# A hybrid attention and delta-rule layer on one core: early embedding and x loads, per-tile normalisation, scan scaling on ACT, and another slab order

## The chip, the core and the metric

The kernel runs on one core of a Trainium2 chip. A core has five engines, each with an in-order instruction queue of its own: TensorE (PE) multiplies matrices, VectorE (DVE), ScalarE (ACT) and GpSimd (POOL) work element by element, and SyncE (SP) issues transfers. They wait for each other through semaphores. The metric is the device time of one execution in microseconds (us); the kernel before takes 786.01 us (median of three runs, 785.57 to 786.49). Everything is in fp32.

## The reference

One layer, sequence 512 and width 1024, batch 1. What is computed, cut to its lines:

```python
h = rms_norm(x, norm_pre)
aq, ak, av, az, dq, dk, dv, db, da, dz, gA, gB = split(h @ w_in)
q = rope(rms_norm(aq, q_norm)); k = rope(rms_norm(ak, k_norm))   # 8 query, 2 key heads of 128
y_att = (softmax(q k^T / sqrt(128)) av * silu(az)) @ w_br_att
cq, ck, cv = silu(short_conv([dq, dk, dv], conv_w))               # 8 heads of 128
g = -exp(a_log) * softplus(da + dt_bias); beta = sigmoid(db)      # forward and backward
o_dn = delta_rule(l2(cq)/sqrt(128), l2(ck), cv, g, beta)          # chunks of 64, both directions summed
y_dn = (rms_norm(o_dn, dn_norm) * silu(dz)) @ w_br_dn             # norm per head
mix = (sigmoid(gA) * y_att + sigmoid(gB) * y_dn) @ w_out
x = x + rms_norm(mix, norm_post)
e = p @ w_ple_proj                                                # the embedding: p is 512 x 256
x = x + rms_norm(sigmoid(x @ w_ple_gate) * e, ple_norm)
```

## The kernel before

**Precision and slabs.** Each fp32 operand is split into a high part, rounded by a cast, and the rest. A product is three matmuls: high by low, low by high, high by high. The combined projection is cut into *slabs* of 128 output columns (dq0 to dq7, dk, dv, dz, az, gA, gB, and later ydn and yatt) and into *blocks* of 512 columns (kv, q0, q1, out0, out1, pg0, pg1). A slab is 8 k-tiles of 3 matmuls over 512 tokens, 24 matmuls (`gemm_t`, L475 to L477). A block's weights come in four pieces, of 24 matmuls each (`gemm_k`, L513 to L515). For each slab and piece `fetch` issues one 512 KB transfer into `wraw`, then ACT casts it into `whi` (1024 columns), and POOL, or DVE, subtracts to get `wlo`. There are two buffers of each of the three. PE's first matmul of a slab reads `wlo` and so waits for all three steps.

**The planner.** The program is written by a planner that runs in Python (class `Flow`, L36 to L130). Every part of the layer is a generator that asks for buffers, events or times; the planner keeps a clock and one list of planned occupied stretches for each engine, always continues the ready part with the smallest priority number (table `PR`), and issues instructions in the planned order, all through L101. Helpers give each instruction its planned duration: `A` for ACT, `V` for DVE, `G` for POOL, `W` for DVE with POOL kept free, `Q` for a transfer. `stream`, the last in priority, works through the slabs in the order of the table `ORDER` and fills whatever PE time the other parts leave. `split` decides by two constants (`COOL`, `HOT`) whether DVE or POOL does a subtraction. What the planner decides is only the order in each queue; on the chip every instruction runs when its semaphores allow.

**The start.** `first_loads` issues the transfers on SP: the norm row, half of p, half of w_ple_proj (`wpp`), the other halves, then the four tiles x0 to x3. `warm_up` (L1708) runs transposes of the identity on PE to fill the time. `h_part` broadcasts the norm row by four matmuls (L347), then squares each x tile on ACT with its sum, takes the inverse root on POOL (`st`), scales with two DVE instructions per tile, and only after all four tiles does it go on to transpose (L374). `ple_part` transposes p (L1171), casts, and runs the product with wpp as eight groups of six matmuls (L1186 to L1188), whose results go to DRAM until the end of the layer.

**The decay and its exponentials.** `decay` (L603 to L676) projects db and da, sums the log decays over a chunk with transposes (L662) and writes the sums to DRAM (`CI`). `prep(g, d)`, for head group g and direction d, reads CI back broadcast over the partitions, masks it on POOL, and takes exponentials on ACT: eight 128x64 activations for each of four chunks (L840), 128 in all. Later it scales them (L860). `make_tables` builds the rope tables on POOL and DVE as soon as the decay is done.

**The scan.** Two groups of four heads run one after the other: `phase_a` (kk and qk products, L884 and L889, and the forward substitution), `phase_b` (the steps in both directions, L1041 to L1093) and `phase_y`. `phase_y(g)` takes the scan output `o` (4 tiles of 128x512, in units `u`), squares it on ACT, sums per head on DVE into `so`, takes the inverse root on POOL (a power with 16 columns, L264, tile `kinv`), scales `o` by it with four 128x512 DVE instructions, and then transposes each head on PE (L1151) and multiplies by the norm weight and the SiLU gate. While it does so, `stream` feeds PE: in group 1 with block q0.

Of the kernel before, what the change touches and what calls it, by code (L numbers as in the profile page):

```python
# [16 lines left out]
NT = 4  # L17
D = 1024
# [120 lines left out]
gB5 dq1 dq2 dk1 dk2 dk6 dq0 dk0 dk3 dq3 dk5 dk7 gB1 dq5 dv0 az4  # L139
dv3 dz2 gB6 gB4 gA1 gB3 dz3 dq4 dv1 dv2 az0 dq7 dz4 dz1 dk4 dq6  # L140
az3 dz7 dz0 dv4 az7 dv5 gA6 gA4 dz6 az6 gB0 kv gB7 dv7 gA7 dv6
gA5 dz5 az2 az5 gA2 q0 gA0 ydn1 q1 gA3 az1 gB2 free_h ydn0 ydn2 ydn6
ydn7 ydn4 ydn5 ydn3 yatt6 yatt4 yatt3 yatt1 vec yatt7 yatt0 yatt5 yatt2 out0 out1 pg0
# [12 lines left out]
def layer(ctx, tc, x, p, wt, wba, wn, wpp, npre, rows, qkn, hd16, npost, pnorm, dnorm, cs, out):  # L156
# [20 lines left out]
    def Q(kb, dep, o, i):  # L177

        t = op("DGE", 0.46, dep, sync.dma_start, o, i)
        return op("DMA", kb * 0.364, t + 0.5, None) + 1.0  # L180
# [111 lines left out]
    def first_loads():  # L292
        yield "get", "u15"
        ple["p"] = unit(15, [128, 4, 256])
        ple["tp"] = []

        def p_half(i):
            ple["tp"].append(Q(2, 0.0, ple["p"][:, 2 * i:2 * i + 2], p[256 * i:256 * i + 256].rearrange("(t p) n -> p t n", p=128)))

        xu = []  # L300

        def ple_weights(half):
            raw = tile("wraw", [128, 2, 512])
            load["ple", half] = raw, Q(4, 0.0, raw, wpp.rearrange("(j p) n -> p j n", p=128)[:, :, half * 512:half * 512 + 512])
            fetched["ple", half].set(F.now)
# [11 lines left out]
        p_half(0)  # L317
        ple_weights(0)
        p_half(1)
# [16 lines left out]
    def h_part():  # L336
# [15 lines left out]
        yield "get", "blk"  # L352
        junk = tile("blk", [128, D])
        for t in range(NT):
            xt, tx = load["x", t]
            ts = A(1.05, tx, act.activation, junk, xt, AF.Square, accum_out=st[:, t:t + 1])
            tj = ts
            ts = rsqrt(1, ts, st[:, t:t + 1], 1.0 / D, EPS)
            for half in range(2):
                xh = xt[:, half * 512:half * 512 + 512]  # L360
                sc[t, half] = ts = V(0.68, max(ts, tn), dve.scalar_tensor_tensor, out=xh, in0=xh, scalar=st[:, t:t + 1],
                                     in1=nb[half], op0=ALU.mult, op1=ALU.mult)
        free("blk", tj)
        free("mm", ts)
        free("mm", ts)
        for t in range(NT):
            xt = load["x", t][0]
            for half in range(2):
                yield "at", sc[t, half] + 0.3
                yield "get", "aux"  # L370
                pt = bank("aux", [128, 4, 128])
                for j in range(4):
                    k = half * 4 + j
                    pe.transpose(pt[:, j, :], xt[:, k * 128:(k + 1) * 128], ident)  # L374
                yield "pe", 0.45
                cc = slice(t * 128, (t + 1) * 128)
                _, te = split(pt, hTh[half][:, :, cc], hTl[half][:, :, cc], F.now, 512)
# [17 lines left out]
        return t  # L395

# [419 lines left out]
    def prep(g, d):  # L816
# [12 lines left out]
        for c in range(NT):  # L829
# [12 lines left out]
            t = A(1.6, t, exps)  # L842
# [284 lines left out]
    def phase_y(g, be):  # L1127
# [9 lines left out]
        for c in range(NT):  # L1137
            t = W(0.62, t, dve.tensor_mul, o[:, c], o[:, c], bc(f[:, c]))
# [22 lines left out]
    def ple_part():  # L1161
# [4 lines left out]
        for t_ in range(NT):  # L1166
            yield "at", ple["tp"][t_ // 2] + 0.2
# [38 lines left out]
    def make_tables():  # L1206

        yield "ev", dec_ev
# [576 lines left out]
def _layout(inputs):  # L1785
# [28 lines left out]
    return {"x": f["x"][0], "p": f["p"][0, 0], "wt": wt, "wba": wba, "wn": wn, "wpp": f["w_ple_proj"][0],  # L1814
# [20 lines left out]
```

## Time and profile before

| what | value |
|---|---|
| median of three runs | 786.01 us (785.57 to 786.49) |
| the profiled execution | 786.52 us |
| its span, first to last instruction | 784.8 us |
| mean granted clock of PE | 0.988 |
| busy: PE / DVE / ACT / POOL | 97% / 60% / 45% / 39% |
| weight casts on ACT | 84, 1050 ns each |
| weight subtractions on POOL | 70, 2401 ns each |
| exponentials on ACT (L840) | 128, 31.7 us in all |

A row of the timeline gives start, duration, engine, line, operation, output and input tiles, shape and count; in brackets the idle time before it and what ended that. A row of the waits gives the waiting instruction, what it waited for, then the sum in us, the number of waits and the longest. A row of windows gives the stretch, its length, the busy time of PE, its weight loads, DVE, ACT and POOL (with instructions), the granted clock as a share of the full one, the DMA share and GB/s. A tile's row gives the shortest, median and longest duration in ns, and the first and last start. Durations of PE's matmuls overlap: what counts there is the step from start to start.

### The profile page before, as it was taken

To read this page: it belongs to the slowest core of one execution; us is meant where nothing else is said; L and a number is where in the kernel's file an instruction comes from. 1 tells how busy PE (TensorE), PEld (TensorE's weight loads), DVE (VectorE), ACT (ScalarE), POOL (GpSimd) and SP (SyncE) were. 2 spreads that over 40 slices of the span, in tenths; PEclk is the share of its full clock that TensorE was granted. 3 is DMA by queue.
4 is the path that set the end of the run, shared out by engine and by line. 5 is a ranking of instruction groups with operands and counts; after the bars stand their busy time and mean duration, and the time that the engine had idled before them with its cause. 6 is when DMAs were issued, how large, how long until landed. Compare 5 with 4: busy or idle time off the path is not lost.

```text
span 784.8 us, 11964 instructions
## 1 busy us (share of the span) xinstructions
PE 760.5 (97%) x4542; PEld 634.1 (81%) x4542; DVE 469.3 (60%) x906; ACT 353.1 (45%) x693; POOL 306.6 (39%) x275
## 2 busy tenths in 40 slices
PE   9999999999999999999999998999999999999995
PEld 6777788788788888888788876787888888888885
DVE  5426868797854769895944554617666744313434
ACT  6568567734441463325432232324557633342422
POOL 4245566303212463203521242656437444562411
PEclk9998999999999999999999998999999999999998
DMA  8362345646202133755231233324233345643313
GB/s 290 123 197 81 134 135 153 196 161 161 95 28 81 54 135 114 208 152 131 98 106 41 81 97 106 121 80 148 81 122 130 116 152 221 228 142 153 94 42 133
DMA packets 54555, 100.51 MB, mean 128 GB/s; under 512 B 21025, under 2 KB 22497, under 8 KB 54498
## 3 DMA queue, kind: packets, MB, share of 16 engines
q1 hardware_dynamic: 54498, 99.75, 39.5%
q8 instruction: 36, 0.59, 0.3%
q14 instruction: 21, 0.17, 0.1%
HBM read 80.83 MB, written 18.91 MB: 127 GB/s over the span
## 4 chain that ended last, share of the span: by engine, by line
PE 70%; DVE 4%; ACT 3%; POOL 2%; issue 2%; DMA 1%; POOLq 0%; DVEq 0%; ACTq 0%; SPq 0%
PE mm L475 12%; PE mm L477 12%; PE mm L476 12%; PE mm L497 4%; PE mm L495 4%; PE mm L496 4%; PE aux L1061 2%; PE mm L1409 2%; PE mm L513 2%; PE mm L514 2%; PE mm L515 2%; PE aux L1093 2%; PE aux L1079 1%; PE aux L1041 1%; PE aux L1052 1%
## 5 line engine op out<-in xcount | busy, mean ns | idle before, releaser
L101 POOL TENSOR_TENSOR wlo<-wraw,whi 128x1024 fp32r<-128x1024 f32 x70 | 168.1, 2401 | 328.4 <-ACT whi L101 317.1
L475 PE MATMUL mm<-u,wlo 128*128 128x512 f32 x576 | 234.0, 406 | 7.5 <-POOL wlo L101 4.4
L477 PE MATMUL mm<-u,whi 128*128 128x512 f32 x576 | 226.2, 393 | 0.0
L476 PE MATMUL mm<-u,whi 128*128 128x512 f32 x576 | 225.6, 392 | 0.0
L101 ACT CAST whi<-wraw 128x1024 fp32r<-128x1024 f32 x84 | 88.2, 1050 | 139.9 <-PE mm L477 70.9
L475 PEld LDWEIGHTS mm<-u,wlo 128*128 128x128 f32 x576 | 109.1, 189 | 28.9 <-POOL wlo L101 6.1
L477 PEld LDWEIGHTS mm<-u,whi 128*128 128x128 f32 x576 | 108.7, 189 | 23.5
L476 PEld LDWEIGHTS mm<-u,whi 128*128 128x128 f32 x576 | 109.1, 189 | 19.9
L101 DVE SCALAR_TENSOR_TENSOR f<-mm,cw,f 128x510 f32<-128x510 f32 (+1 forms) x96 | 71.9, 749 | 34.7 <-ACT f L101 32.1
L495 PE MATMUL mm<-u,u 128*128 128x512 f32 (+1 forms) x136 | 52.0, 383 | 0.0
L497 PE MATMUL mm<-u,u 128*128 128x512 f32 (+1 forms) x136 | 51.4, 378 | 0.0
L496 PE MATMUL mm<-u,u 128*128 128x512 f32 (+1 forms) x136 | 51.2, 377 | 0.0
L101 DVE TENSOR_TENSOR u<-aux,u 128x512 f32<-128x512 f32 (+1 forms) x56 | 37.5, 688 | 20.4 <-ACT u L101 16.8
L101 POOL TENSOR_TENSOR u<-wraw,u 128x1024 fp32r<-128x1024 f32 x16 | 38.3, 2402 | 14.5 <-ACT u L101 14.3
L513 PE MATMUL mm<-whi,u 128*128 128x512 f32 x96 | 38.9, 405 | 0.0
L514 PE MATMUL mm<-wlo,u 128*128 128x512 f32 x96 | 38.3, 398 | 0.0
L515 PE MATMUL mm<-whi,u 128*128 128x512 f32 x96 | 38.2, 397 | 0.0
L101 ACT COPY c<-aux 128x512 f32<-128x512 f32 x18 | 10.6, 590 | 54.6 <-DVE f L101 30.9
L840 ACT ACTIVATE u<-u,cj 128x64 f32<-128x64 f32 x128 | 31.7, 334 | 6.5 <-POOL u L101 6.5
L101 ACT ACTIVATE f<-mm 128x512 f32<-128x512 f32 (+1 forms) x36 | 20.1, 571 | 21.4 <-PE mm L497 8.4
L497 PEld LDWEIGHTS mm<-u,u 128*128 128x128 f32 x136 | 25.6, 188 | 4.8
L496 PEld LDWEIGHTS mm<-u,u 128*128 128x128 f32 x136 | 25.6, 188 | 4.6
(245 smaller groups left out, 1260.9 us busy)
## 6 DMA issues: line engine op xcount, KB each, us to landing
wraw<-in_wt_dram SPq DMA_DIRECT2D x72, 512.0 KB, 3.4
wraw<-in_wn_dram SPq DMA_DIRECT2D x28, 512.0 KB, 4.0
u<-CI SPq DMA_DIRECT2D x16, 256.0 KB, 4.8
u<-in_x_dram SPq DMA_DIRECT2D x4, 512.0 KB, 7.6
eD<-c SPq DMA_DIRECT2D x8, 256.0 KB, 2.6
gate_gB<-go SPq DMA_DIRECT2D x8, 256.0 KB, 2.1
gate_az<-go SPq DMA_DIRECT2D x8, 256.0 KB, 2.0
gate_dz<-go SPq DMA_DIRECT2D x8, 256.0 KB, 2.3
```

The source lines that it names most:

```text
L101: fn(*a, **k)
L475: pe.matmul(o, lo[:, k, :], mh(k), start=(k == 0), stop=False)
L476: pe.matmul(o, hi[:, k, :], ml(k), start=False, stop=False)
L477: pe.matmul(o, hi[:, k, :], mh(k), start=False, stop=(k == 7))
L495: pe.matmul(o, b, hi, start=(i == 0), stop=False)
L496: pe.matmul(o, a, lo, start=False, stop=False)
L497: pe.matmul(o, a, hi, start=False, stop=(i == 7))
L513: pe.matmul(o[t], b, hi, start=(k == 0), stop=False)
L514: pe.matmul(o[t], a, lo, start=False, stop=False)
L515: pe.matmul(o[t], a, hi, start=False, stop=(k == 7))
L840: act.activation(e, e, AF.Exp, bias=cj[:, d, c, 4 * g + h, i:i + 1])
L1061: pe.matmul(pw[:, h, :], Vm[g][d][:, 4 * c + h, :], r[:, h, :], start=True, stop=True)
```

## The change

- **First loads.** p is stored so that each partition's row is one run of 4 KB and comes in one transfer; each half of wpp is stored as contiguous 4 KB rows too. SP issues: norm row, p, both halves of wpp, x0 to x3. A planned transfer now costs 0.3 us per KB of a row and 1.3 behind it, before 0.364 and 1.0.
- **x_norm.** The normalisation is a part of its own. It sets an event for each x tile, and `h_part` transposes a tile as soon as that tile is scaled.
- **phase_y.** The scaling of `o` is sixteen 128x128 activations on ACT with a scale per partition (L1141), where it was four 128x512 multiplications on DVE. The planner gives four of them 1.15 us, and eight exponentials 1.64 for 1.6.
- **Tables.** `make_tables` waits for both directions of group 0's exponentials to be scaled and no longer for the decay alone.
- **Constants.** New `ORDER`, `OUT0`, `PR`; `WARM` 8.4 for 9; `COOL` 1.5 for 2.5. The matmuls are the same in number and shape; there are 21 warm-up transposes and not 20.

```diff
 ORDER = """
-gB5 dq1 dq2 dk1 dk2 dk6 dq0 dk0 dk3 dq3 dk5 dk7 gB1 dq5 dv0 az4
+dq0 dq3 gB0 dq1 dk1 dq2 dk0 dk2 dk3 dv2 dz4 dk4 dk7 dz3 dv3 dv0
...
-PR = dict(dec=5, dm1=2, y=2, conv=1, gate=3, kv=9, q=8, head=8, ple=2, prep=9, tab=11)
+PR = dict(dec=7, dm1=11, y=4, conv=6, gate=0, kv=9, q=6, head=0, ple=11, prep=4, tab=7)
...
-WARM = 9
+WARM = 8.4
-COOL, HOT = 2.5, -3
+COOL, HOT = 1.5, -3
...
-        return op("DMA", kb * 0.364, t + 0.5, None) + 1.0
+        return op("DMA", kb * 0.3, t + 0.5, None) + 1.3
...
-            load["ple", half] = raw, Q(4, 0.0, raw, wpp.rearrange("(j p) n -> p j n", p=128)[:, :, half * 512:half * 512 + 512])
+            load["ple", half] = raw, Q(4, 0.0, raw, wpp[half])
...
-        p_half(0)
+        ple["tp"] = Q(4, 0.0, ple["p"], p)
         ple_weights(0)
-        p_half(1)
...
+        spawn(x_norm(sc, sc_ev, nb, tn), 0)
         for t in range(NT):
             xt = load["x", t][0]
+            yield "ev", sc_ev[t]
...
+    def x_norm(sc, sc_ev, nb, tn):
+        yield "get", "blk"
+        junk = tile("blk", [128, D])
+        for t in range(NT):
+            xt, tx = load["x", t]
+            yield "at", tx - 0.4
+            ts = A(1.05, tx, act.activation, junk, xt, AF.Square, accum_out=st[:, t:t + 1])
+            tj = ts
+            ts = rsqrt(1, ts, st[:, t:t + 1], 1.0 / D, EPS)
+            for half in range(2):
+                xh = xt[:, half * 512:half * 512 + 512]
+                sc[t, half] = ts = V(0.68, max(ts, tn), dve.scalar_tensor_tensor, out=xh, in0=xh, scalar=st[:, t:t + 1],
+                                     in1=nb[half], op0=ALU.mult, op1=ALU.mult)
+            sc_ev[t].set(F.now)
...
         for c in range(NT):
-            t = W(0.62, t, dve.tensor_mul, o[:, c], o[:, c], bc(f[:, c]))
+            def scaled(c=c):
+                for h in range(4):
+                    act.activation(o[:, c, h], o[:, c, h], AF.Copy, scale=f[:, c, h:h + 1])
+
+            t = A(1.15, t, scaled)
...
-        yield "ev", dec_ev
+        yield "ev", E_ev[0, 0]
+        yield "ev", E_ev[0, 1]
         yield "get", "f2"
...
-    return {"x": f["x"][0], "p": f["p"][0, 0], "wt": wt, "wba": wba, "wn": wn, "wpp": f["w_ple_proj"][0],
+    return {"x": f["x"][0], "p": f["p"][0, 0].reshape(4, 128, 256).transpose(1, 0, 2), "wt": wt, "wba": wba, "wn": wn, "wpp": f["w_ple_proj"][0].reshape(2, 128, 2, 512).transpose(2, 1, 0, 3),
```

How the queues stand at the places where the orders differ most. A row is a line of the kernel, the operation, output and input tiles and the shape; `x8` is eight alike. First ACT, at the first exponentials of group 0. In before, `whi_521` is the high part of slab dk1, `whi_570` that of dk2 and `whi_648` that of dk6:

```order
L101 CAST whi_521<-wraw_412 128x1024
L101 ACTIVATE f_78_523<-mm_459,cw 128x512
L101 ACTIVATE mm_459<-f_78_523 128x512
L840 ACTIVATE u_73_499<-u_73_499,cj 128x64 x8
L840 ACTIVATE u_74_500<-u_74_500,cj 128x64 x8
L840 ACTIVATE u_73_499<-u_73_499,cj 128x64 x8
L101 CAST whi_570<-wraw_495 128x1024
L101 ACTIVATE f_83_572<-mm_524,cw 128x512
L840 ACTIVATE u_74_500<-u_74_500,cj 128x64 x8
L101 ACTIVATE f_88_615<-mm_610 128x512
L101 CAST whi_648<-wraw_553 128x1024
```

In the changed kernel `whi_550` is the high part of dk1 and the cast behind the last row below is that of dq2 (`go_552` is a gate's activation):

```order
L841 ACTIVATE u_66_468<-u_66_468,cj 128x64 x8
L841 ACTIVATE u_67_469<-u_67_469,cj 128x64 x8
L101 CAST whi_550<-wraw_464 128x1024
L101 ACTIVATE go_552<-mm_496 128x512
L841 ACTIVATE u_66_468<-u_66_468,cj 128x64 x8
L841 ACTIVATE u_67_469<-u_67_469,cj 128x64 x8
L101 ACTIVATE f_81_593<-mm_588 128x512
L841 ACTIVATE u_66_468<-u_66_468,cj 128x64 x8
L841 ACTIVATE u_67_469<-u_67_469,cj 128x64 x8
L841 ACTIVATE u_66_468<-u_66_468,cj 128x64 x8
```

In before the 24 exponentials stand ahead of dk2's cast; now 16 stand ahead of dk1's and 40 more ahead of dq2's, and slabs dq0, dq3, gB0 and dq1 come before them. Next ACT at phase_y(1), before (`f_604` to `f_607` are the squares; `whi_4493` and `whi_4525` are pieces 3 and 4 of q0, `u_608_4445` takes the transposed heads):

```order
L101 ACTIVATE f_604_4441<-u_518_3954 128x512
L101 ACTIVATE f_605_4442<-u_518_3954 128x512
L101 ACTIVATE f_606_4443<-u_518_3954 128x512
L101 ACTIVATE f_607_4444<-u_518_3954 128x512
L101 CAST whi_4493<-wraw_4383 128x1024
L101 CAST whi_4525<-wraw_4459 128x1024
L101 CAST u_608_4445<-mm_4531 128x512
```

and now (`whi_4501` and `whi_4538` are pieces 3 and 4 of q0):

```order
L101 ACTIVATE f_604_4446<-u_524_4018 128x512
L101 ACTIVATE f_605_4447<-u_524_4018 128x512
L101 ACTIVATE f_606_4448<-u_524_4018 128x512
L101 ACTIVATE f_607_4449<-u_524_4018 128x512
L101 CAST whi_4501<-wraw_4405 128x1024
L1141 ACTIVATE u_524_4018<-u_524_4018,kinv 128x128 x16
L101 CAST whi_4538<-wraw_4485 128x1024
```

The sixteen activations stand between the casts of pieces 3 and 4. Last PE, at the first transpose of phase_y(1), before:

```order
L513 MATMUL mm_4453<-whi_4424,u_11_127 128x512
L514 MATMUL mm_4453<-wlo_4425,u_9_125 128x512
L515 MATMUL mm_4453<-whi_4424,u_9_125 128x512
L1151 MATMUL mm_4531<-ident,u_518_3954 128x128 x4
L513 MATMUL mm_4450<-whi_4493,u_12_128 128x512
L514 MATMUL mm_4450<-wlo_4494,u_10_126 128x512
```

and now:

```order
L514 MATMUL mm_4458<-whi_4501,u_12_128 128x512
L515 MATMUL mm_4458<-wlo_4502,u_10_126 128x512
L516 MATMUL mm_4458<-whi_4501,u_10_126 128x512
L1156 MATMUL mm_4580<-ident,u_524_4018 128x128 x4
L514 MATMUL mm_4455<-whi_4538,u_12_128 128x512
L515 MATMUL mm_4455<-wlo_4539,u_10_126 128x512
```

Before, the first transpose stood behind pieces 1 and 2 of q0 (48 matmuls behind the last scan step); now it stands behind piece 3 (72 of q0 and 6 of slab gB3).

More of the change, by code (lines that the diff above doesn't have):

```diff
@@ L138 @@
 ORDER = """
-gB5 dq1 dq2 dk1 dk2 dk6 dq0 dk0 dk3 dq3 dk5 dk7 gB1 dq5 dv0 az4
[L140 to L143, printed above, removed]
-pg1
-"""
-OUT0 = 'ydn5 ydn3 yatt6 yatt4'
-PR = dict(dec=5, dm1=2, y=2, conv=1, gate=3, kv=9, q=8, head=8, ple=2, prep=9, tab=11)
+dq0 dq3 gB0 dq1 dk1 dq2 dk0 dk2 dk3 dv2 dz4 dk4 dk7 dz3 dv3 dv0
+gA5 dz7 dk6 gA3 gB4 az6 dz2 az5 gA2 dv1 dq5 dq4 gA1 dk5 dq6 dq7
+dz0 az2 gA7 dz1 az0 dv7 gB1 dv4 vec az1 az3 dz5 gA0 kv dv5 gB7
+dv6 gA4 gB5 az4 gB6 gB3 q0 dz6 gA6 q1 az7 gB2 free_h ydn6 ydn4 ydn7
+ydn0 ydn2 ydn5 ydn3 ydn1 yatt0 yatt3 yatt4 yatt1 yatt2 yatt7 yatt6 yatt5 out0 out1 pg0
+pg1
+"""
+OUT0 = 'ydn7 ydn3 ydn3 yatt3'
+PR = dict(dec=7, dm1=11, y=4, conv=6, gate=0, kv=9, q=6, head=0, ple=11, prep=4, tab=7)
 GAP = 0.0
 X_DVE = ()
-WARM = 9
+WARM = 8.4
 W1 = 0
-COOL, HOT = 2.5, -3
+COOL, HOT = 1.5, -3
 @with_exitstack
@@ L294, in first_loads @@
         ple["p"] = unit(15, [128, 4, 256])
-        ple["tp"] = []
-        def p_half(i):
-            ple["tp"].append(Q(2, 0.0, ple["p"][:, 2 * i:2 * i + 2], p[256 * i:256 * i + 256].rearrange("(t p) n -> p t n", p=128)))
         xu = []
@@ L351, in h_part @@
         sc = {}
[L352 to L365, printed above, removed]
+        sc_ev = [Event() for _ in range(NT)]
+        spawn(x_norm(sc, sc_ev, nb, tn), 0)
         for t in range(NT):
             xt = load["x", t][0]
+            yield "ev", sc_ev[t]
             for half in range(2):
@@ L395, in h_part @@
         return t
+    def x_norm(sc, sc_ev, nb, tn):
[12 more added lines that the diff above has]
+            sc_ev[t].set(F.now)
+        free("blk", tj)
+        free("mm", ts)
+        free("mm", ts)
     slab, blocks, fetched = {}, {}, {}
@@ L840, in exps @@
                         act.activation(e, e, AF.Exp, bias=cj[:, d, c, 4 * g + h, i:i + 1])
-            t = A(1.6, t, exps)
+            t = A(1.64, t, exps)
             if away:
@@ L1166, in ple_part @@
         for t_ in range(NT):
-            yield "at", ple["tp"][t_ // 2] + 0.2
+            yield "at", ple["tp"] + 0.2
             yield "get", "mm"
```

## The prediction

> **What bounds the kernel now.** The page comes first, for which engine is full; then the waits of TensorE (PE), for where it is not; then windows and the timeline around the two largest waits, for who is late there. On the page:
>
> ```profile
> span 784.8 us, 11964 instructions
> PE 760.5 (97%) x4542; PEld 634.1 (81%) x4542; DVE 469.3 (60%) x906; ACT 353.1 (45%) x693; POOL 306.6 (39%) x275
> PEclk9998999999999999999999998999999999999998
> ```
>
> PE is busy for 97% of the span; no other engine reaches two thirds. The change leaves the matmuls alone but for one warm-up transpose more, so it can only add or take away time in which PE stands still, and time in which its clock is low: the PEclk row has three eights (the 4th, the 25th and the last slice). PE's waits, largest first:
>
> ```profile
> PE mm L475 <- POOL wlo L101: 4.4, 2, 3.7
> PE mm L1151 <- DVE u L101: 3.7, 3, 2.4
> PE mm L475 <- POOL saq L272: 1.9, 2, 1.2
> PE aux L972 <- issue: 1.1, 2, 0.6
> ```
>
> The two top waits are the two places where the clock falls:
>
> ```profile
> 40.00:60.00 20.00, 16.97 (x86) 13.96 (x85) 5.08 (x8) 12.65 (x44) 9.22 (x9) 0.98 0.69 193
> 60.00:80.00 20.00, 19.29 (x80) 15.71 (x81) 12.94 (x19) 16.53 (x49) 10.50 (x9) 0.85 0.27 83
> 460.00:480.00 20.00, 16.14 (x61) 12.41 (x60) 11.02 (x12) 4.88 (x7) 9.46 (x8) 0.83 0.47 152
> 59.31:66.14 6.83, 5.43 (x13) 4.26 (x14) 3.75 (x6) 6.83 (x25) 4.89 (x4) 0.50 0.33 92
> 472.32:479.15 6.83, 5.33 (x13) 4.08 (x14) 3.37 (x4) 0.58 (x1) 0.77 (x1) 0.50 0.38 122
> ```
>
> The column behind the five busy times is the granted clock, as a mean. The last two rows frame the fall: half speed for 6.83 us, of which PE had work for 5.4, so 2.7 us lost each time, beside the wait itself. **Place one**, ACT and then POOL:
>
> ```profile
> 41.94 0.27 PE L662 MATMUL aux<-ident,f 128*64 128x128 f32 x1
> 51.39 5.83 ACT L840 ACTIVATE u<-u,cj 128x64 f32<-128x64 f32 x24
> 57.13 1.03 ACT L101 CAST whi<-wraw 128x1024 fp32r<-128x1024 f32 x1
> 58.31 2.35 POOL L101 TENSOR_TENSOR wlo<-wraw,whi 128x1024 fp32r<-128x1024 f32 x1 [1.02 <-ACT whi L101]
> 60.71 0.79 PE L475 MATMUL mm<-u,wlo 128*128 128x512 f32 x1 [3.74 <-POOL wlo L101]
> ```
>
> The first row is the transpose of the summed decays, from which the exponentials' inputs go through DRAM and back. The exponentials stand in ACT's in-order queue ahead of the cast of slab dk2's weights; cast and subtraction follow, and PE has waited 3.74 us. **Place two**, the per-head norm of the second scan (phase_y(1)):
>
> ```profile
> 457.25 1.16 PE L1093 MATMUL aux<-c,u 128*128 128x128 f32 x8
> 460.33 2.20 ACT L101 ACTIVATE f<-u 128x512 f32<-128x512 f32 x4 [1.48 <-DVE u L1102]
> 464.20 2.90 POOL L264 TENSOR_TENSOR kinv<-kinv,pw 128x16 f32<-128x16 f32 x1
> 467.36 2.38 POOL L101 TENSOR_TENSOR wlo<-wraw,whi 128x1024 fp32r<-128x1024 f32 x1
> 467.43 6.81 DVE L101 TENSOR_TENSOR u<-u,kinv 128x512 f32<-128x512 f32 x4 [3.97 <-POOL kinv L101]
> 470.53 2.56 POOL L101 TENSOR_TENSOR wlo<-wraw,whi 128x1024 fp32r<-128x1024 f32 x1 [0.79 <-ACT whi L101]
> 463.73 0.39 PE L513 MATMUL mm<-whi,u 128*128 128x512 f32 x1
> 468.94 0.39 PE L515 MATMUL mm<-whi,u 128*128 128x512 f32 x1
> 470.44 0.30 PE L1151 MATMUL mm<-ident,u 128*128 128x128 f32 x1 [1.11 <-DVE u L101]
> 470.95 0.33 PE L1151 MATMUL mm<-ident,u 128*128 128x128 f32 x1 [0.21 <-DVE u L101]
> 473.69 1.08 PE L1151 MATMUL mm<-ident,u 128*128 128x128 f32 x2 [2.42 <-DVE u L101]
> ```
>
> From the last scan step (457.25) on: squares, sums, a power on POOL, then four scalings on DVE in 6.81 us, of which the transposes wait for the first three; PE's cover, 48 matmuls of q0, ends before them. From 463.73 to 468.94 are 23 steps: 0.2265 us for each 128x512 matmul, 5.4 for a slab of 24.
>
> **The change, part by part.**
>
> *phase_y's scale from DVE to ACT.* Four DVE instructions go for sixteen 128x128 activations. What they cost is shown by the tile's summary (min/median/max in ns) and by sixteen activations of the same shape:
>
> ```profile
> L101 DVE TENSOR_TENSOR u<-u,kinv x8: 677/688/2878, 294.2 to 473.6; 128x512 f32<-128x512 f32 x8
> 272.11 4.77 ACT L860 ACTIVATE u<-u,Nj 128x128 f32<-128x128 f32 x16
> ```
>
> So ACT takes 4.8 us where DVE took 6.81, and would take 4 x 0.688 = 2.75 if nothing ran beside it; two of its four stretched while POOL's wlo (467.36 and 470.53) ran. [...] I take the 6.81, for POOL subtracts beside it in the new order too: the chain is 2.0 us shorter.
>
> What hides it matters more. In the new order PE has 6 matmuls of gB3 and 72 of q0 behind the last scan step before the first transpose, 78 x 0.2265 = 17.7 us against 48 x 0.2265 = 10.9; the scan step itself is 1.0 more (457.25 to 469.17, the end of the 48, less 10.9). The chain from that step on, by the rows above: 10.2 us until kinv is there (467.43 less 457.25), as before; then 4.8 of ACT: 15.0. PE comes to the transposes at 18.7: no wait, 3.7 us of slack. Also ACT's cast of q0's block 4 stands behind the sixteen: cast to 16.1, subtraction 2.4, 18.5, while PE wants it behind the first transposes, at about 19.1; block 3 is cast ahead of them and comes in time by some half a microsecond. So the 1.11+0.21+2.42 and the 0.4 of the slower steps between go, and with them the 2.7 of low clock: **-7.1 us** (bounds: 0, if the chain is 7 us later than I count, and -7.1).
>
> phase_y(0): ACT has 4 squares, 12 decay activations (12/16 x 4.77 = 3.6) and the sixteen ahead of az0's cast. From the last scan step: kinv at 10.2 and sixteen to 15.0, a cast and a subtraction (1.05 + 2.4), 18.5, or 20.5 if the twelve hold the sixteen up by 2 us. PE has 51 large matmuls until then (11.6 us) and 8.4 of small ones, 20.0. So 0 to 1.5 with the slack of a gate's activation: taken **+0.5**.
>
> *New slab order at place one.* All 64 exponentials of group 0 still run in this stretch. In ACT's new queue the cast for dk1 stands behind 16 of them, the one for dq2 behind 16+24 = 40. At 5.83/24 = 0.243 us each, from the transpose at L662 (L663 after): first exponential +9.45 (51.39 less 41.94, as before), 16 exps 3.9, cast and tanh 1.5, 16 exps 3.9, a square 0.5, 24 exps 5.8, cast 1.05, subtraction with a mask step ahead of it 2.7: +28.7. PE has until then the rest of dq3, gB0, dq1, dk1 (2.0 + 3 x 5.4 = 18.3), 18 matmuls of the embedding (4.1) and some 2.5 of small ones and transposes: +25. It waits **3.6 us** at dq2, as it waits 3.74 at dk2 now; dk1 itself comes within 0.5 of its turn. The exchange is nearly even, clock included.
>
> *p, w_ple_proj and x at the start.* These are the rows:
>
> ```profile
> 2.88 3.78 PE L347 MATMUL mm<-blk,ones 1*128 1x512 f32 x4
> 10.97 1.06 ACT L101 ACTIVATE blk<-u 128x1024 f32<-128x1024 f32 x1
> 11.70 0.47 PE L1186 MATMUL mm<-u,u 128*128 128x512 f32 x1
> 13.97 5.35 DVE L101 SCALAR_TENSOR_TENSOR u<-u,st,mm 128x512 f32<-128x512 f32 x8
> 26.80 0.42 PE L604 MATMUL mm<-u,f 128*64 128x512 f32 x1 [0.22 <-ACT u L101]
> u<-in_x_dram SPq DMA_DIRECT2D x4, 512.0 KB, 7.6
> ```
>
> One issue fewer and longer rows bring x0 down some 1.6 us sooner, by my count of the issues. But the first square (10.97) does not wait for x0: ahead of it in ACT's queue stand the casts of p's transposes, and those wait for PE, which has 8 warm-ups (6 before) and the 3.78 us of the norm row's broadcast first. The square stays near 10.9. Thereafter the per-tile events let x0 be transposed while x3 is still to be squared, so the decay starts near 24.8 and not at 26.80: -2.0. But five of eight embedding groups are done by then; the other 18 matmuls (4.1 us) come later, and PE's idle stretches between the transposes (2.3 us) are inside the 24.8. Together **+2.1**; less 0.4 us of small stalls (0.22 in the decay row, the rest beside it) that the new fill covers: **+1.7**. Bounds: -2 (x's lead is used after all, since rows show x landing late, 7.6 us from issue) and +3.
>
> *Tables later.* make_tables leaves POOL and DVE when the group-0 exponentials need them, and comes with dz3 to dv0. In before one short wait for a subtraction remains beside the 3.7 (4.4-3.7 = 0.7, at dv3); in the new place the weights of dv3 and dv0 come 1.5 and 0.6 us ahead of PE: **-0.6** (bounds -0.7 and +1.5).
>
> *The rest of the order.* Slabs of the same size in other places: the casts and subtractions behind them are as many per slab in the scan, the attention and the output as before, so waits such as the 1.9 behind saq and the 1.1 of issue are kept at their price: **0** (bounds -2 and +2).
>
> **Sum**: -7.1 + 0.5 - 0.1 (3.6 for 3.74) + 1.7 - 0.6 = -5.6. The profiled execution ran 786.52 us (span 784.8 and 1.7 around it), the median of the runs shown is 786.01. I take the median: 786.0 - 5.5 = **780.5 us**.
>
> On the clock, since it decides 2.7 us at dq2: both long waits of before halved it, and the fall at 59.31 came 2.4 us after the wait began (60.71 less 3.74 is 56.97). [...]
>
> **The rivals.**
>
> *A: the wait at dq2 is shorter, or leaves the clock at full speed.* For it: the exponentials begin when their inputs come back from DRAM, and the head is 2 us ahead. Against: 40 of them stand before one cast. 780.5 - 2.7 = 777.8. Chance 0.2.
>
> *B: x's early landing is used.* If ACT gets to x0 at its landing, the head gains 2 instead of losing 1.7: 780.5 - 3.7 = 776.8. Against: the queue above. 0.15.
>
> *C: ACT becomes the gate (slower).* Place: the casts behind activations on ACT. If ACT's sixteen end 4.2 us later than I count at phase_y(1), block 4 of q0 uses up its 0.6 of slack, PE waits 3.6 and halves its clock again: 7.1 gained there is 6.3 given back; with az0's wait at 1.5 (1.0 above my 0.5) and 3 at the head (1.3 above): 780.5 + 6.3 + 1.0 + 1.3 = 789.1. [...] For it: a cast behind 4.8 us of activations, with 0.6 us of slack. Against: the wait must grow by a row that I have not seen. 0.18.
>
> *D: the change does not do what it says at phase_y(1).* If POOL's subtractions ahead of the power, or a cast ahead of the squares, make that chain 6 us longer, the 3.7 us of slack are gone, PE waits 2.3 and the clock falls: 780.5 + 2.3 + 2.7 = 785.5. Against: in the new queues nothing of that size stands there. 0.09.
>
> **How the numbers follow.** My forecast, within 2 us of 780.5, has 0.38. A measurement of this kernel can tell 0.2% (1.6 us) from no change. Faster: forecast, A and B, 0.38 + 0.2 + 0.15 = 0.73, less 0.01 for ends near the bound: 0.72. Same: D and that end, 0.10. Slower: C, 0.18. The range takes in B with its bound (776.8 less 2.3) and D and half of C: 774.5 to 788.
>
> **What would show it.** In the profile after: no PE wait for the transposes of phase_y(1), and full clock in the slice around 470; a wait of 3 to 4 us on wlo near 65 us with the clock low behind it; the decay's first matmul near 24.8; the first square near 10.9. Wrong would be: a long wait at q0's block 4 or az0, a first square at x0's landing (near 8.5), or a new stall of several us where I have put 0, in the scan or the attention.

## The result, and the profile after

The changed kernel takes 777.45 us (median of four runs, 777.38 to 778.91), the kernel before beside it 785.79: ratio 0.9897, 95% interval 0.988 to 0.9914, so 8.3 us less. Forecast were 5.5 us less and 780.5 (774.5 to 788.0). The profiled executions have spans of 775.7 and 784.8 us, 9.1 us apart; the profiled execution of before took 786.5 us, at the upper end of its runs, so that terms read from the two profiles add to 9.1 and not to 8.3.

The page of the changed kernel:

```profile
span 775.7 us, 11989 instructions
PE 756.2 (97%) x4543; PEld 631.2 (81%) x4543; DVE 462.5 (60%) x902; ACT 360.0 (46%) x719; POOL 302.3 (39%) x274
PEclk9999999999999999999999999999999999999998
```

The eights of the 4th and the 25th slice are gone from the clock row. PE's waits and the same windows as before:

```profile
PE mm L476 <- POOL wlo L101: 3.0, 1, 3.0
PE mm L476 <- POOL saq L272: 2.4, 2, 1.2
...
PE mm L1156 <- DVE u L101: 0.5, 1, 0.5
```

```profile
40.00:60.00 20.00, 20.00 (x95) 16.49 (x95) 6.96 (x11) 16.39 (x53) 9.65 (x10) 1.00 0.68 208
60.00:80.00 20.00, 17.03 (x72) 13.60 (x71) 11.88 (x17) 13.50 (x36) 7.13 (x3) 0.91 0.29 96
460.00:480.00 20.00, 20.00 (x93) 16.38 (x92) 3.16 (x5) 10.41 (x23) 10.95 (x8) 1.00 0.41 132
```

From 460 to 480 us PE is now busy without a gap at full clock (16.14 us at 0.83 before). One long wait is left, between 60 and 80. Here it is, on ACT, POOL and PE:

```profile
57.59 5.84 ACT L841 ACTIVATE u<-u,cj 128x64 f32<-128x64 f32 x24
63.33 1.04 ACT L101 CAST whi<-wraw 128x1024 fp32r<-128x1024 f32 x1
64.51 2.35 POOL L101 TENSOR_TENSOR wlo<-wraw,whi 128x1024 fp32r<-128x1024 f32 x1 [6.74 <-ACT whi L101]
66.91 0.50 PE L476 MATMUL mm<-u,wlo 128*128 128x512 f32 x1 [2.97 <-POOL wlo L101]
```

The chain is the old one with slab dq2 in the place of dk2: exponentials, cast, subtraction, and PE behind them. Then phase_y(1):

```profile
453.29 0.94 PE L1094 MATMUL aux<-c,u 128*128 128x128 f32 x7
...
461.00 2.90 POOL L264 TENSOR_TENSOR kinv<-kinv,pw 128x16 f32<-128x16 f32 x1
464.24 4.79 ACT L1141 ACTIVATE u<-u,kinv 128x128 f32<-128x128 f32 x16 [2.02 <-POOL kinv L101]
468.94 1.04 ACT L101 CAST whi<-wraw 128x1024 fp32r<-128x1024 f32 x1
470.05 2.38 POOL L101 TENSOR_TENSOR wlo<-wraw,whi 128x1024 fp32r<-128x1024 f32 x1 [3.49 <-ACT whi L101]
471.98 0.60 PE L1156 MATMUL mm<-ident,u 128*128 128x128 f32 x4
472.65 0.39 PE L515 MATMUL mm<-wlo,u 128*128 128x512 f32 x1
```

The first row shows seven of the eight matmuls of the last scan step, which starts at 453.18. The scaling ends at 469.0, 15.9 us behind it (forecast 15.0), and PE comes to the transposes at 471.98, 18.8 behind it (forecast 18.7), with no bracket behind the row: it did not wait. The low part of piece 4's weights is ready at 472.4, and the first matmul that reads it starts at 472.65: 0.2 us of slack are left.

### The profile page after: what moved, and what is told of

Read it like the earlier page. It is cut to its first block, busy times and chain, and to the rows that moved or that the text cites. A ratio compares the mean times of both kernels' runs of the same rounds, so it can differ in the third digit from the quotient of the medians.

```text
span 775.7 us, 11989 instructions
## 1 busy us (share of the span) xinstructions
PE 756.2 (97%) x4543; PEld 631.2 (81%) x4543; DVE 462.5 (60%) x902; ACT 360.0 (46%) x719; POOL 302.3 (39%) x274
## 4 chain that ended last, share of the span: by engine, by line
PE 80%; ACT 7%; DVE 6%; DMA 2%; issue 2%; POOL 2%; SPq 0%; POOLq 0%; DVEq 0%; ACTq 0%
PE mm L476 14%; PE mm L478 14%; PE mm L477 14%; PE mm L496 4%; PE mm L498 4%; PE mm L497 4%; DVE f L101 3%; ACT u L841 2%; PE mm L515 2%; PE mm L516 2%; PE mm L514 2%; PE aux L1062 2%; PE mm L1415 2%; PE aux L1094 2%; PE aux L1080 1%
## 5 line engine op out<-in xcount | busy, mean ns | idle before, releaser
L101 POOL TENSOR_TENSOR wlo<-wraw,whi 128x1024 fp32r<-128x1024 f32 x68 | 162.6, 2392 | 288.2 <-ACT whi L101 275.8
L101 DVE SCALAR_TENSOR_TENSOR f<-mm,cw,f 128x510 f32<-128x510 f32 (+1 forms) x96 | 71.9, 749 | 21.2 <-ACT f L101 18.7
L498 PE MATMUL mm<-u,u 128*128 128x512 f32 (+1 forms) x136 | 51.4, 378 | 0.0
L514 PE MATMUL mm<-whi,u 128*128 128x512 f32 x96 | 38.0, 396 | 0.0
L516 PE MATMUL mm<-whi,u 128*128 128x512 f32 x96 | 37.4, 390 | 0.0
L101 ACT ACTIVATE mm<-f 128x512 f32<-128x512 f32 x24 | 14.4, 600 | 39.3 <-DVE f L101 39.3
L498 PEld LDWEIGHTS mm<-u,u 128*128 128x128 f32 x136 | 25.6, 188 | 4.9
```

Source lines behind the costliest of these rows:

```text
L101: fn(*a, **k)
L498: pe.matmul(o, a, hi, start=False, stop=(i == 7))
L514: pe.matmul(o[t], b, hi, start=(k == 0), stop=False)
L516: pe.matmul(o[t], a, hi, start=False, stop=(k == 7))
```

## The experiments

The question is what carried the 7 us at phase_y(1), the engine that scales, PE's cover, or the slab order, and whether the other terms of the sum are what they were said to be. Times are compared by their ratio to the kernel before, run beside each. Where two kernels have the same order on PE, "lag" is the difference between the starts of the same PE instruction in their two traces.

**The changed kernel with the scaling on DVE.** Queues otherwise as they are.

```diff
             def scaled(c=c):
-                for h in range(4):
-                    act.activation(o[:, c, h], o[:, c, h], AF.Copy, scale=f[:, c, h:h + 1])
+                dve.tensor_mul(o[:, c], o[:, c], bc(f[:, c]))
```

> The changed kernel with phase_y's scale given back to DVE, four 128x512 multiplications at the same places of the program, every queue otherwise as in the changed kernel. Theory (the gain at phase_y(1) comes from PE's cover, 78 matmuls ahead of the first transpose where there were 48, and not from the engine that scales): DVE needs 2.75 us alone and 6.8 at worst, the transposes have more than 3 us of slack, so the time stays at the changed kernel's, 777.5 within 0.8 us, and no wait over 0.6 us stands at the transposes of group 1. Rival (ACT is what pays, because DVE and POOL stretch each other): 4 to 7 us come back, 781.5 to 784.5.

779.4 us, ratio 0.9914 (0.9896 to 0.9932): by the ratios about 1.3 us slower than the changed kernel, more than the 0.8 that the theory allowed and far from the rival's 4 to 7. Its waits have one that the changed kernel lacks, and the scaling of group 1 is long again:

```profile
PE aux L890 <- DVE u L101: 1.3, 1, 1.3
```

```profile
465.96 6.88 DVE L1140 TENSOR_TENSOR u<-u,kinv 128x512 f32<-128x512 f32 x4 [3.98 <-POOL kinv L101]
```

At group 1 DVE took 6.88 us, as long as in before, and no wait appeared there: PE's cover hid it. The lag comes at 294 us, 1.4 us, in phase_y(0): one of the four multiplications there took 2.9 us ahead of a DVE step that PE's next product needs. Another 0.3 comes at 485 us, in the wait behind saq, the tile of POOL's inverse root behind q0. So ACT is worth some 1.4 us in the first group and takes away no wait at the transposes of the second, once the cover is there.

**The kernel before with the scaling on ACT.** PE's order as before.

```diff
-            t = W(0.62, t, dve.tensor_mul, o[:, c], o[:, c], bc(f[:, c]))
+            def scaled(c=c):
+                for h in range(4):
+                    act.activation(o[:, c, h], o[:, c, h], AF.Copy, scale=f[:, c, h:h + 1])
+
+            t = W(0.62, t, scaled)
```

> The kernel before with phase_y's scale as sixteen activations on ACT at the same places of the program, planned durations unchanged, so that PE's order is the one of before (48 matmuls ahead of the first transpose). Cover theory: the chain ends 10.2 + 4.8 = 15.0 us behind the last scan step and PE is there at 11.9, so some 3 us of waiting stay where 4.1 were, and the clock still falls: 784 to 786. Rival (the engine pays): the wait and the fall of the clock go, 778 to 780.

783.87 us, ratio 0.9973 (0.9959 to 0.9988), 2.1 us faster. Its timeline at phase_y(1), and the window in which the clock fell in before:

```profile
468.56 4.79 ACT L1140 ACTIVATE u<-u,kinv 128x128 f32<-128x128 f32 x16 [2.42 <-POOL kinv L101]
470.29 0.38 PE L1155 MATMUL mm<-ident,u 128*128 128x128 f32 x2
471.36 0.33 PE L1155 MATMUL mm<-ident,u 128*128 128x128 f32 x1 [0.69 <-ACT u L1140]
472.52 0.33 PE L1155 MATMUL mm<-ident,u 128*128 128x128 f32 x1 [0.84 <-ACT u L1140]
```

```profile
469.25:472.67 3.42, 1.89 (x11) 1.22 (x9) 0.00 (x0) 3.42 (x14) 1.62 (x1) 1.00 0.23 51
```

The total is 0.1 us below the cover theory's range, but not for its reason. Only 1.5 us of waiting stay, for the transposes follow the scaling tile by tile and need 13 of the 16 activations, and the clock does not fall (1.00 in the window; the mean of the execution is 0.992, before 0.988). By the lag this place gains 5.1 us. Given back are 1.2 at 300 us, where two casts wait behind the activations of phase_y(0), 0.8 behind q0 and 0.3 near 594 us; 2.9 us are left between the spans of the two profiles. So the engine does carry much at phase_y(1) in the old order, against my theory, and it pays for it where ACT's queue is the one that PE waits for.

**The kernel before with the scaling planned longer, and on DVE alone.** `W` keeps POOL free in the plan while DVE works, `V` does not; the instructions are the same.

```diff
-            t = W(0.62, t, dve.tensor_mul, o[:, c], o[:, c], bc(f[:, c]))
+            t = V(1.15, t, dve.tensor_mul, o[:, c], o[:, c], bc(f[:, c]))
```

> The kernel before with one line changed: each of phase_y's four multiplications stays on DVE, but is planned at 1.15 us on DVE alone, before 0.62 on DVE with POOL kept free. The planner then puts 69 matmuls of q0 ahead of the first transpose and not 48; loads, slab order and all else are as before. Cover theory: PE comes to the transposes 16.6 us behind the last scan step, DVE's third multiplication was done at 16.4 in before, so nearly all of the wait and the fall of the clock go: 778.5 to 780.5. Rival (ACT or the slab order pays): 784 or more.

783.92 us, ratio 0.9971 (0.9956 to 0.9986): 2.3 us faster, where the theory had 6 to 8. The first transposes wait no longer (472.40, with DVE again at 6.9 us), but a new wait stands behind the third head:

```profile
482.38 0.47 PE L475 MATMUL mm<-u,wlo 128*128 128x512 f32 x1 [2.29 <-DVE u L101]
```

By the trace's order, the slab behind q0 asks for a result bank while q0's four results and a transposed head hold all five, and DVE frees them one by one. The cover, alone, turns one wait into another.

The edit changes two things, and the planner tells them apart. The order in which it issues PE's instructions has 48 matmuls ahead of the first transpose of group 1 in before, 69 with this edit, 66 with 0.62 planned on DVE alone, and still 48 with 1.15 planned with POOL kept free. So 18 of the 21 more come from no longer reserving POOL, and the longer duration alone brings none. In the changed kernel it is alike: 78, and 72 with 0.62 on ACT, but 54 with 0.62 on DVE and POOL. None of these other plans was timed.

**The same with dz6 behind q0.** In the changed kernel's order dz6 stands behind q0, and the third head's transpose needs its gate. Here dz6 and ydn1 are moved in the old order:

```diff
-            t = W(0.62, t, dve.tensor_mul, o[:, c], o[:, c], bc(f[:, c]))
+            t = V(1.15, t, dve.tensor_mul, o[:, c], o[:, c], bc(f[:, c]))
...
-az3 dz7 dz0 dv4 az7 dv5 gA6 gA4 dz6 az6 gB0 kv gB7 dv7 gA7 dv6
-gA5 dz5 az2 az5 gA2 q0 gA0 ydn1 q1 gA3 az1 gB2 free_h ydn0 ydn2 ydn6
+az3 dz7 dz0 dv4 az7 dv5 gA6 gA4 az6 gB0 kv gB7 dv7 gA7 dv6
+gA5 dz5 az2 az5 gA2 q0 dz6 gA0 q1 gA3 az1 gB2 free_h ydn1 ydn0 ydn2 ydn6
```

> The kernel before with phase_y's four multiplications planned longer on DVE alone, and with two entries of the slab order moved: dz6 from ahead of the scan's end to right behind q0, ydn1 from ahead of q1 to the other ydn slabs. The plan then puts 69 matmuls ahead of the first transpose, and the third and fourth transposes into q1, as in the changed kernel. Theory (the second wait of 2.3 us in the run with the longer plan alone comes from three transposed heads and q0's four results holding all five banks; spreading them takes it away): no wait over 1 us from 466 to 500, 2 to 3 us less than that run's 783.9: 781 to 782. Rival (the wait only moves again): 783 to 785.

784.16 us, ratio 0.9984 (0.9974 to 0.9993), in the rival's range. From 466 to 483 us the wait of 2.3 is gone and none over 0.3 is left, as the theory said; the time did not follow. Its waits:

```profile
PE mm L475 <- POOL wlo L101: 5.5, 3, 4.3
PE mm L475 <- POOL saq L272: 2.4, 2, 1.2
PE mm L475 <- DVE f L101: 1.7, 1, 1.7
```

The wait at dk2 was 4.3 us here (3.7), the one at the end of kv 1.7 (1.0), one of 0.7 is new at a yatt slab (644.64), and the mean clock of the profiled execution was 0.991 (0.994 with the longer plan alone). The first grew with the way of the decays through DRAM, whose order the edit leaves alone: the first mask behind it started at 50.93 us (49.46 in before), the 24 exponentials at 51.60 (51.39), and they took 6.03 (5.83). At kv the edit has a hand in it: dz6 stood ahead of kv, so kv now comes one slab earlier, and eight transposes on DVE (367.68 to 373.42) now stand between its products, where in before they stand ahead of them all. That this is what grew the second wait is my reading. The mechanism at phase_y(1) is shown, the sum is not.

**The changed kernel with the old constants** (order, priorities, warm-up, thresholds).

```diff
-dq0 dq3 gB0 dq1 dk1 dq2 dk0 dk2 dk3 dv2 dz4 dk4 dk7 dz3 dv3 dv0
+gB5 dq1 dq2 dk1 dk2 dk6 dq0 dk0 dk3 dq3 dk5 dk7 gB1 dq5 dv0 az4
...
-PR = dict(dec=7, dm1=11, y=4, conv=6, gate=0, kv=9, q=6, head=0, ple=11, prep=4, tab=7)
+PR = dict(dec=5, dm1=2, y=2, conv=1, gate=3, kv=9, q=8, head=8, ple=2, prep=9, tab=11)
...
-WARM = 8.4
+WARM = 9
-COOL, HOT = 1.5, -3
+COOL, HOT = 2.5, -3
```

> The changed kernel with the old tables of constants (slab order, priorities, warm-up, thresholds). Its plan has 72 matmuls ahead of the first transpose of group 1, and 32 exponentials ahead of dk2's cast where before had 24. Theory: the phase_y gain of 7 us stays, the wait at dk2 grows by about 2 us and the start is near the old one: 779 to 782. Rival (the new slab order carries the gain): 784 or more.

800.06 us, ratio 1.0177 (1.0155 to 1.0199): 14 us slower than before. The theory's 779 to 782 failed outright; the rival had said 784 or more. Waits and the tables' transfers of this run:

```profile
PE mm L476 <- POOL wlo L101: 8.7, 5, 5.4
PE mm L476 <- DVE f L101: 6.4, 1, 6.4
PE mm L476 <- DVE u L101: 3.8, 3, 2.3
```

```profile
L101 SPq DMA_DIRECT2D TAB<-blk x2: 326/326/327, 387.0 to 392.9; - x2
```

The 5.4 is at dk2, behind 32 exponentials. The 6.4 is at 385 us: with the new event and the old priority the tables are made at 387 to 393 us, where the key tails need them (123 to 129 in the changed kernel, 82 to 88 in before). That kv's results then hold the banks is my reading of the trace and was not tested.

**The kernel before with the new constants.** Nothing else: the same lines the other way round.

```diff
-gB5 dq1 dq2 dk1 dk2 dk6 dq0 dk0 dk3 dq3 dk5 dk7 gB1 dq5 dv0 az4
+dq0 dq3 gB0 dq1 dk1 dq2 dk0 dk2 dk3 dv2 dz4 dk4 dk7 dz3 dv3 dv0
...
-PR = dict(dec=5, dm1=2, y=2, conv=1, gate=3, kv=9, q=8, head=8, ple=2, prep=9, tab=11)
+PR = dict(dec=7, dm1=11, y=4, conv=6, gate=0, kv=9, q=6, head=0, ple=11, prep=4, tab=7)
```

> The kernel before with only the new tables of constants (slab order, priorities, warm-up, thresholds); loads, normalisation, phase_y and tables as before. Its plan has 54 matmuls between the last scan step and the first transpose of group 1 (48 before, 78 in the changed kernel) and 48 exponentials ahead of dq2's cast. Theory (the constants and the edits of the code need each other): PE reaches the transposes 13.2 us behind the last scan step, DVE's third multiplication came at 16.4, so some 3 us of waiting and the fall of the clock stay, and the wait at dq2 is 4 to 6 us: 784 to 790. Rival (the slab order alone carries the gain): 777 to 780.

786.92 us, ratio 1.001 (1.0 to 1.0019), as expected. There is a wait at each of the two places:

```profile
PE mm L710 <- DVE u L101: 5.3, 2, 5.1
PE mm L1151 <- DVE u L101: 4.2, 5, 2.4
```

The first stands not at dq2's weights but at the transposes right ahead of dq2 (67.20); dq2's own weights come at 68.4. With the old event and the new priorities, POOL makes the tables among the masks of the exponentials here (47.36 to 58.2), where before makes them at 78.5 to 87.3: part of this wait may belong to the tables' event. The new constants alone gain nothing, and the new code without them loses 14 us. The two halves work only together.

**Later exponentials.** Sets of eight that nobody waits for are issued later on ACT, plan untouched.

```diff
+LATE = {(0, 0, 2): 8.0, (0, 1, 2): 8.0, (0, 0, 3): 14.0, (0, 1, 3): 14.0}
...
-            heapq.heappush(self.later, (t, self.n, fn, a, k))
+            heapq.heappush(self.later, (t + late, self.n, fn, a, k))
...
-            t = A(1.64, t, exps)
+            t = A(1.64, t, exps, late=LATE.get((g, d, c), 0.0))
```

> The changed kernel with four of group 0's eight sets of eight exponentials issued 8 to 14 us later in ACT's queue, so that 32 and not 48 stand ahead of dq2's cast; the plan and PE's order are untouched. Theory (PE's 3.0 us wait at dq2 and the clock behind it come from those exponentials): the weights come 3.9 us sooner, wait and fall of the clock go, 3.0 + 1.7 = 4.7 us less than the changed kernel: 772 to 774 where the changed kernel has 777.5. Rival (dq2 waits for its transfer, or the exponentials only block the next slab later): 776.5 to 778.

773.98 us, ratio 0.9848 (0.9835 to 0.986): 3.8 us faster than the changed kernel by the ratios. dq2's cast and first matmul:

```profile
57.68 1.04 ACT L102 CAST whi<-wraw 128x1024 fp32r<-128x1024 f32 x1
...
63.86 0.39 PE L478 MATMUL mm<-u,wlo 128*128 128x512 f32 x1
```

In the changed kernel 56 exponentials stand ahead of that cast (16, 16 and 24), and 32 here; the 48 of the expectation were miscounted. The cast comes 5.6 us sooner, the time of 24 exponentials, and PE goes on without a wait; the lag there is -4.6, of which two new waits of 0.4 to 0.5 us give back 0.9.

**The wait filled with transposes.** Same wait, PE kept busy.

```diff
         o = bank("mm")
+        if name == ("dq", 2):
+            for _ in range(26):
+                pe.transpose(o[:, 0:128], ident, ident)
```

> The changed kernel with 26 transposes of the identity on PE (0.106 us each, 2.8 us) ahead of dq2's first matmul, into the bank that this gemm then overwrites; they fill the wait of 3.0 us. Theory (beside the wait itself the half clock behind it costs 1.7 to 2.7 us): the clock stays full after 63 us, the weights come as before: 1.4 to 2.4 us less than the changed kernel, 775 to 776. Rival (the clock costs nothing there because PE would wait for the next weights anyway): no change, 777 to 778.

776.32 us, ratio 0.9871 (0.9857 to 0.9885): 2.0 us faster than the changed kernel by the ratios, 1.1 by the medians. The mean clock of the profiled execution is 0.998, in the changed kernel 0.995. Behind dq2 the profile is 1.6 us ahead of the changed kernel's. So of the 4.7 us at dq2 the wait is 3.0 and the clock 1.7.

**p and w_ple_proj in the old rows.**

```diff
-            load["ple", half] = raw, Q(4, 0.0, raw, wpp[half])
+            load["ple", half] = raw, Q(4, 0.0, raw, wpp.rearrange("(j p) n -> p j n", p=128)[:, :, half * 512:half * 512 + 512])
-        ple["tp"] = Q(4, 0.0, ple["p"], p)
+        ple["tp"] = Q(4, 0.0, ple["p"], p.rearrange("(t p) n -> p t n", p=128))
...
-    return {"x": f["x"][0], "p": f["p"][0, 0].reshape(4, 128, 256).transpose(1, 0, 2), "wt": wt, "wba": wba, "wn": wn, "wpp": f["w_ple_proj"][0].reshape(2, 128, 2, 512).transpose(2, 1, 0, 3),
+    return {"x": f["x"][0], "p": f["p"][0, 0], "wt": wt, "wba": wba, "wn": wn, "wpp": f["w_ple_proj"][0],
```

> The changed kernel with p and w_ple_proj stored and loaded as before, in rows of 1 KB and 2 KB (p still in one transfer), issues in the same order and all queues else the same. Theory (x's earlier landing is not used, since ACT's first square stands behind the casts of p's transposes): x lands up to 1.3 us later than in the changed kernel, the first square stays within 0.3 us of 10.6, and the time within 0.5 us of the changed kernel's. Rival (the 4 KB rows pay through x): 1 to 1.6 us slower, 778.5 to 779.1.

777.15 us, ratio 0.9887 (0.9869 to 0.9905): no difference, though the six runs spread from 775.51 to 779.45. x0 landed at 9.2 us instead of 8.7 (10.0 in before), and the first square stood at the same place:

```profile
10.62 1.07 ACT L101 ACTIVATE blk<-u 128x1024 f32<-128x1024 f32 x1
```

**Less warm-up.** The kernel with later exponentials, three of the first eight warm-up transposes left out.

```diff
+        i = 0
         while F.now < WARM:
-            pe.transpose(o, ident, ident)
+            if i not in (5, 6, 7):
+                pe.transpose(o, ident, ident)
+            i += 1
```

> The changed kernel with the later exponentials and three of the first eight warm-up transposes left out. The norm row's broadcast on PE then starts 0.4 us sooner, and the casts of p's transposes and the first square with it. Theory (the start hangs on PE's queue and ACT's behind it): the first square near 10.2, the decay's first matmul near 23.7, and the time 0.3 to 0.5 us below the run with the later exponentials alone, 773.5. Rival (x or the norm row's transfer sets the start): the same as that run, 774.0.

773.74 us, ratio 0.9851 (0.9837 to 0.9865), not told apart from 773.98 by time. The trace shows the step:

```profile
9.98 1.08 ACT L102 ACTIVATE blk<-u 128x1024 f32<-128x1024 f32 x1
...
23.56 0.47 PE L607 MATMUL mm<-u,f 128*64 128x512 f32 x1
```

Square and decay are 0.6 us sooner (10.62 and 24.13 without the edit). x0 landed at 8.8, 1.1 us ahead of the square, so the start moves with PE's first instructions. This kernel and the one with the later exponentials are the fastest versions found, both below the changed kernel.

**The tables back at the end of the decay.**

```diff
-        yield "ev", E_ev[0, 0]
-        yield "ev", E_ev[0, 1]
+        yield "ev", dec_ev
```

> The changed kernel with make_tables back at the end of the decay; the planner then puts 8 table products (0.70 us each) and two scalings on POOL among the masks of the first exponentials, and shifts what follows. Theory: masks and exponentials come 1 to 3 us later, the wait at dk1 or dq2 grows by as much: 778 to 782. Rival (the tables have room on POOL, the event does nothing): 776.5 to 778.

779.13 us, ratio 0.9918 (0.9902 to 0.9934): 1.6 us slower. The wait on the weights in the exponentials' stretch is 0.9 longer, and stands at dk0 and no longer at dq2:

```profile
PE mm L476 <- POOL wlo L101: 3.9, 1, 3.9
```

This is not the old place of the tables: POOL makes them at 46.1 to 57.1 us here, among the masks, and in before at 78.5 to 87.3, behind group 0's exponentials. So the run prices the old event under the new priorities.

**The scaling of phase_y(1) doubled.** Four more activations behind the four of each tile.

```diff
                 for h in range(4):
                     act.activation(o[:, c, h], o[:, c, h], AF.Copy, scale=f[:, c, h:h + 1])
+                if g == 1:
+                    for h in range(4):
+                        act.activation(o[:, c, h], o[:, c, h], AF.Copy, scale=1.0)
```

> The changed kernel with sixteen more activations of the same shape (scale 1, the values stay) behind the sixteen of phase_y(1), so that ACT has 9.6 us there; all queues else the same. This puts the prediction's slower rival to the test. By the trace of the changed kernel the scaling ends at 469.0 and the first transpose comes at 472.0, and q0's piece 4 gets its weights at 472.4, when PE wants them: 0.1 us of slack. Theory: the transposes wait some 2 us, piece 4 is 4.8 us late, PE stands still 4.7 us in all and the clock falls for one or two stretches of 3.4 us: 5 to 7.5 us slower than the changed kernel, 782 to 785. Other theory (ACT's scaling has room to spare): under 2 us slower.

781.19 us, ratio 0.9941 (0.9924 to 0.9958), about 3.5 us slower than the changed kernel; the profiled execution is 5.6 behind. Half a microsecond at the first matmul of piece 4 for its high part, and then

```profile
PE mm L515 <- POOL wlo L101: 1.9, 1, 1.9
```

with a mean clock of 0.992 in the profiled execution (0.995 in the changed kernel). The transposes did not wait: the last scalings end at 471.0, and PE comes at 471.6. ACT was busy with the 32 activations for 8.0 us (463.84 to 471.84) and not for the expected 9.6, since four of the extra ones took 0.89 us and four scalings 1.27; so the price is below the expected one. The place is the one that the slower rival named: the cast of piece 4 behind ACT's activations.

## Why the prediction held, and which terms were off

The number lies in the range, but 3 us below the forecast and outside the 2 us around it that had the chance of 0.38. What held is the course of it: the large gain at phase_y(1), a wait that stays at dq2, a lost microsecond at the start.

**phase_y(1), -7.1.** Right in place and size, though the terms written for it (1.11, 0.21, 2.42, 0.4 and 2.7) add to 6.8: the three waits and the fall of the clock are gone, 0.5 us came back at the last transpose. The two reasons given, a shorter scaling and a longer cover, were both there, and the runs show that each alone takes away most of it (5.1 us by the engine, all of the first waits by the cover), and that each alone brings a new price elsewhere, so that either gains only 2 us in all. What I had not put into the sum is the order behind q0, which spreads the transposes over the banks. Where the cover comes from I had left to the slab order. Most of it comes from the plan of the scaling, which no longer reserves POOL: with the new order and the old plan there are 54 matmuls ahead of the first transpose, with the new plan 78.

**dq2, 3.6 us with 2.7 of half clock.** The mechanism was right and both sizes were too large: 2.97, and one stretch of half clock where I had two:

```profile
64.93:68.34 3.41, 1.43 (x6) 1.21 (x7) 3.00 (x4) 3.41 (x12) 2.33 (x2) 1.00 0.12 24
68.34:71.76 3.42, 3.42 (x10) 2.67 (x9) 3.26 (x5) 1.05 (x3) 1.98 (x1) 0.50 0.66 231
```

PE came there 25.1 us behind the transpose of the decays, as counted, and the weights 28.0 behind it. The terms in the prediction add to 28.8 and 24.9, so the 3.6 should have read 3.9. Against before (3.74 and 2.7) this is 1.8 us of gain, for which the sum had 0.1. It is the largest term that was mis-sized. Of the 1.8, 1.0 is one stretch of half clock instead of two, and that differs from one execution to the next: with the old rows a wait of 3.0 cost two (last section). The clock fell here after a stretch of 3.41 us in which PE was busy for 1.43, in before at 59.31 after one with 1.07. (The 2.4 us that the prediction puts between the start of before's wait and that fall are 2.3: 59.31 less 56.97.)

**The start, +1.7.** Measured at the transpose of the summed decays, with the work still to do:

```profile
10.62 1.07 ACT L101 ACTIVATE blk<-u 128x1024 f32<-128x1024 f32 x1
13.54 0.66 PE L357 MATMUL aux<-ident,u 128*128 128x128 f32 x4 [0.64 <-DVE u L101]
24.02 0.47 PE L605 MATMUL mm<-u,f 128*64 128x512 f32 x1
38.85 0.27 PE L663 MATMUL aux<-ident,f 128*64 128x128 f32 x1
```

38.85 plus 4.1 for the 18 postponed matmuls is 42.95 against 41.94: +1.0. The steps held: the square at 10.62 (forecast 10.9), five groups done before the decay, x's lead unused (shown by the old rows), the decay at 24.02 for 24.8. Rival B is refuted.

**az0, +0.5.** It was 0: PE did not wait there. **Tables, -0.6.** The wait at dv3 (0.65) is gone, but the reason given was wrong: in before POOL makes the tables at 78.5 to 87.3 us, behind group 0's exponentials (51.4 to 70.8), so moving them could not free the engines for these, and the wait at dv3 stands at 142.65. What took it away is not shown, and that the size fits is luck. **The rest, 0.** A wait of 0.36 at 90 us and 0.7 between 207 and 233 went, 0.2 at kv came, and the waits behind saq grew from 1.9 to 2.4: about -0.4. Together: -6.6 (7.1 less 0.5) -1.8 +1.0 -0.65 -0.4 = -8.45, beside 9.1 between the spans; 0.6 are not assigned. The forecast's own terms add to -5.6, of which it took 5.5.

**A** came half true, and its 777.8 is the number nearest to the measured one: the wait at dq2 was shorter, and the clock fell all the same, but for one stretch. **The slower rival** named the right place, and the slack there was 0.2 us and not 0.6. The doubled scaling gives its price: 3.5 us. **D** did not occur.

## What to carry to other kernels

Where a planner or a hand-written order sets the queues, what a step reserves in the plan is also a promise of cover: planning four steps on one engine, and no longer on two, moved the transposes 18 matmuls later, and with the longer duration 21, which the profile shows as a wait that is gone. A step moved to another engine is paid in that engine's queue, by the casts behind it; look there, and at the order behind the moved consumers, for what is late next. And a wait on the engine that bounds the kernel can cost its length plus the clock, so filling it is worth something even where it cannot be removed: 1.6 us here, behind a wait of 3.0.

## What the runs showed of the hardware

The changed kernel's trace has the granted clock from 10.32 us on: full to 68.34, half to 71.76 and full to 771.49 us, which are 17, 1 and 205 times 3.413 us. That of before has it from 11.53 on: full to 59.31, half to 66.14, full to 472.32, half to 479.15 and full to 779.52, which are 14, 2, 119, 2 and 88 times 3.413. The wait at dq2 cost one stretch of half clock in the changed kernel's profile (2.97 us) and two with the old rows (3.0):

```profile
62.53:65.94 3.41, 1.41 (x7) 0.83 (x5) 1.61 (x3) 3.41 (x11) 1.44 (x1) 1.00 0.21 77
65.94:69.35 3.41, 2.45 (x6) 1.96 (x7) 3.01 (x5) 3.41 (x8) 2.33 (x2) 0.50 0.41 124
69.35:72.77 3.42, 3.42 (x10) 2.65 (x9) 2.57 (x4) 0.03 (x1) 0.96 (x1) 0.50 0.65 238
```

Cut into such steps, the two kernels' profiles have half clock behind those with PE busy for 1.05 us (before, 468.91 to 472.32), 1.07 (before, 55.90 to 59.31) and 1.43 (changed, 64.93 to 68.34), and at the end of the kernel behind 0.84 (before) and none (changed); all their other steps at full clock have PE busy for 2.13 us or more, and full clock behind them. Half clock went on behind steps with 1.91 and 2.01 us (before, from 472.32 and 59.31) and 2.45 (old rows), and ended behind those with 3.42 (both kernels). That the place of the steps decides how many stretches of half clock, 1.7 us each, one and the same wait costs is my reading of these rows. It fits the spread of the runs: the changed kernel's four lie within 1.5 us, and the six with the old rows lie at 775.5 to 775.9 with a mean clock of 0.996 to 0.997, or at 778.4 to 779.5 with 0.993.

In before, three of DVE's eight multiplications by `kinv` took 2.82 to 2.88 us. They began at 296.01, 467.43 and 470.82, while POOL subtracted (295.64 to 298.34, 467.36 to 469.74, 470.53 to 473.09); the other five, which began while it did not, took 0.68 to 0.69. In the run with the scaling on DVE the eight took 0.68 to 2.91. ACT's scaling shows no such stretch beside the same subtraction (464.16 to 466.55 us in the changed kernel): 386 to 402 ns in all 32 instructions.
